# Ten weight blocks of a decoder trunk in products of seven, with the PSUM halves' role change moved

## The chip, the cores and the metric

The kernel runs on one core of a Trainium2 chip. The metric is the device time of one execution in microseconds, as the median of several runs. PE is TensorE (PEld its weight loads), DVE is VectorE, ACT is ScalarE, POOL is GpSimd, SP is SyncE, whose queue here issues the weight loads.

## The reference

One layer on 256 tokens of width 2048, all in float32. The input is normalised; one matrix `w_in` makes three branches' inputs and the gates; each branch's output of width 1024 goes through its own projection, is gated and summed; `w_out`, a scaled residual and a LayerNorm follow; then a SwiGLU feed-forward part (FFN) of width 5632 with its own residual and LayerNorm.

```python
x = layer_norm(x, ln_in_g, ln_in_b)
z = jnp.einsum('bsd,de->bse', x, w_in[l])
a_b, a_c, a_h, b_u, b_v, c_a, c_g, g = jnp.split(z, SPLITS, axis=-1)
gates = jax.nn.sigmoid(g + gate_bias[l]).reshape(bsz, s, N_BRANCH, D_MODEL)
y_a = short_gated_conv(a_b, a_c, a_h, conv_a_w[l])          # a_b * conv3(a_c * a_h)
y_b = chunked_spatial_gating(b_u, b_v, ...)                  # b_u * (W_group @ layer_norm(b_v) + b)
y_c = conformer_conv(c_a, c_g, ...)                          # silu(layer_norm(conv31(c_a * sigmoid(c_g))))
proj = jnp.einsum('bsnc,ncd->bsnd', ys, w_branch[l])
merged = jnp.sum(gates * proj, axis=2)
x = layer_norm(DEEPNORM_ALPHA * x + einsum(merged, w_out[l]), ln_mix_g[l], ln_mix_b[l])
h_gate, h_up = split(einsum(x, w_ffn_in[l]))
x = layer_norm(DEEPNORM_ALPHA * x + einsum(silu(h_gate) * h_up, w_ffn_out[l]), ...)
```

## The kernel before

**Products.** Activations stand transposed, so that 128 rows of the contraction (a k tile) lie on the partitions. The 256 tokens are two halves of 128 (`t`). Every float32 operand is split into a high and a low part (`whi`, `wlo` for weights, `th`, `tl` or `yh`, `yl` for activations): ACT casts the high part (L126), DVE subtracts it (L128). One product of a 128 x 128 activation block and a 128 x 512 weight block is three matmuls, high by high, high by low and low by high (L203 to L205, L247 to L249).

**Chunks and blocks.** The weights come in raw tiles of 512 KB, loaded on SP's queue in the order of a plan (L86 to L118). A chunk is 512 columns: a raw tile holds two k tiles, and a step of `gemm` (L220) uses one raw tile with both token halves, 12 matmuls. A block is 1024 columns as two halves `n`: a raw tile holds one k tile, and a plain step of `gemm_block` (L251) makes four products, again 12 matmuls. A block may have pairs: two raw tiles, that is a 2 x 2 of weight blocks, for which `split_pair` (L131) forms sums on DVE and splits seven weight operands, and PE makes seven products of them with sums of activations that `token_sums` (L780) has made before. Four of a pair's products go to four further PSUM banks, `shared`; after the last pair DVE forms from these what is added to each output (L291 to L296), and `total` (L805) adds it when the output is read. Pairs come after at most six plain steps (`LEAD`). Before the change only FFN blocks have pairs: three in those of `w_ffn_in`, two in those of `w_ffn_out` (called fo below).

**Loading ahead.** `pump` (L190) runs at each step: it loads up to five raw tiles ahead, splits three ahead, and takes up to two items from `background`, a list with the 31 taps of the long convolution on DVE (L536). There are four raw buffers and seven buffers for split weights.

**PSUM.** Eight banks form two halves of four. `acc_bank` takes from the first, `tp_bank` (transposes, L301) from the second, and `halves.reverse()` at the end of a chunk or block exchanges their roles. Transposes are mostly deferred by some steps with `defer` (L210), and `run_deferred` runs them when due.

**Skew.** Some chunks run the second token half a few steps behind the first (`SKEW` is 5): w_out's last chunk, and the first chunk of the FFN. When w_out's last chunk ends for a token half, `evac_o` (L760) adds the residual into `R`, takes statistics, normalises (L429), transposes (L305) and splits the result into `x2T`.

**Order of the stages.** cg, ca (twice), bv, bu, then for branch B four gate chunks and four projection chunks, then ac, ah, ab (twice), branch A and branch C in the same way, four w_out chunks, then the FFN in three parts. In branch C, `finish_c` (L558) normalises the convolution's output after the second gate chunk. `residual` (L749) loads a quarter of x again and normalises it into temporary tiles, one w_out chunk ahead of its use.

**Order of the instructions.** The code is written for a framework that orders each engine's instructions when the program is built, by priority of the code's order and by estimated times: an instruction whose operands are estimated late is passed by a later one. So taps or residual pieces can stand ahead of where the code has them. It also allocates the buffers and sets the waits.

Of the kernel before, what the change touches and what calls it, by code (L numbers as in the profile page):

```python
# [14 lines left out]
P = 128  # L15
D = 2048
# [24 lines left out]
H_PAIRS = 2  # L41
LEAD = 6
# [9 lines left out]
def trunk_kernel(ctx: ExitStack, tc: tile.TileContext, x, ln_in_g, ln_in_b, w_in, gate_bias,  # L52
# [78 lines left out]
    def split_pair(t0, t1):  # L131
# [3 lines left out]
        ts = ffp.tile([P, 3, NW], F32, name="tsum", bufs=1)  # L135
# [74 lines left out]
    def defer(fn, after=DEFER):  # L210

        deferred.append((clock[0] + after, fn))
# [38 lines left out]
    def gemm_block(key, xs, evac, combos=None):  # L251
# [7 lines left out]
        adds, shared = {}, None  # L259
# [7 lines left out]
        for s_, (kind, q, tile_) in enumerate(steps):  # L267
# [9 lines left out]
            else:  # L277
# [11 lines left out]
                if sp:  # L289
# [59 lines left out]
    for j in range(2):  # L349
        for nm, off in (("ac", OFF_AC), ("ah", OFF_AH), ("ab", OFF_AB)):  # L350
            plan_in(nm, off, j)
    plan_branch(BR_A)
    plan_branch(BR_C)
    for j in range(4):
# [25 lines left out]
    wT = cwp.tile([P, 8, P], F32, name="wT")  # L380
# [63 lines left out]

    xT = new_xt(act)
    def x_stats(t):
# [5 lines left out]
    def x_norm(t, q):  # L452
        mu, rs = x_ms[t]
        norm_transposed(xT, q, t, xt[t][:, cols(q)], mu, rs, PR_ING, PR_INB, new_tmp(), act=ACT_BLOCKS[t])
# [21 lines left out]
    b_ln = []  # L476

    def more_params():
# [12 lines left out]
        for b0 in range(0, 8, 4):  # L491
            tp = transpose4(sgw[:, b0:b0 + 4, :])
            nc.scalar.copy(out=wT[:, b0:b0 + 4, :], in_=tp)
        xin.close()
        brp = br.enter_context(tc.tile_pool(name="brp", bufs=1))
        for src in (sg_ln_g, sg_ln_b):
# [4 lines left out]
    defer(more_params)  # L501
# [81 lines left out]
    vt = {(t, j): brp.tile([P, NW], F32, name="gate", bufs=8) for t in range(NT) for j in range(2)}  # L583
# [18 lines left out]
    for j in range(2):  # L602
        def evac_bu(t, ps, j=j):
# [3 lines left out]
            def later():  # L607
                mx = tp_bank()
                for b in range(4):
                    nc.tensor.matmul(mx[:, b, :], lhsT=wT[:, 4 * j + b, :], rhs=vt[t, j][:, cols(b, P)],  # L610
# [13 lines left out]
    def branch(n, y, first, prepare=None, mT=None):  # L624
        gates = {}
        for j in range(4):
            gb = brp.tile([P, NW], F32, name="gb", bufs=2)
            o = n * D + j * NW
            nc.scalar.dma_start(out=gb, in_=gate_bias[0:1, o:o + NW].broadcast_to([P, NW]))

            def evac_g(t, ps, j=j, gb=gb):
                g = brp.tile([P, NW], F32, name="gate", bufs=8)
                nc.vector.tensor_tensor(out=g, in0=ps, in1=gb, op=ALU.add)
                nc.scalar.activation(out=g, in_=g, func=AF.Sigmoid)
                gates[j, t] = g

            gemm(("g", n, j), xT, evac_g)
            if j == 1 and prepare is not None:
                defer(prepare)
        if mT is not None:  # L640
            mT.extend(new_xt(act))
        for j in range(4):
            def evac_p(t, ps, j=j):
                m = merged[t][:, cols(j)]
                if first:
                    nc.vector.tensor_tensor(out=m, in0=ps, in1=gates[j, t], op=ALU.mult)
                else:
                    z = gates[j, t]
                    nc.vector.tensor_tensor(out=z, in0=ps, in1=z, op=ALU.mult)
                    nc.vector.tensor_tensor(out=m, in0=m, in1=z, op=ALU.add)  # L650
                if mT is not None:
                    defer(lambda: split_to(mT, 4 * j, t, transpose4(blocks(m))), 2)

            gemm(("p", n, j), y, evac_p)

    branch(BR_B, yb, True)


    ya = new_y()

    def branch_a_chunk(j):
        ac, st = {}, {}

        def evac_ac(t, ps):
            ac[t] = new_tmp()
            nc.scalar.copy(out=ac[t], in_=ps)

        gemm(("ac", j), xT, evac_ac)

        def evac_ah(t, ps):  # L670
            u = ac[t]
            nc.vector.tensor_tensor(out=u, in0=ps, in1=u, op=ALU.mult)

            def later():
                if t == 0:
                    st["pad"] = brp.tile([P, 4, KC - 1 + S], F32, name="pad", bufs=2)
                    nc.vector.memset(st["pad"][:, :, 0:KA - 1], 0.0)
                tp = transpose4(blocks(u))
                pad = st["pad"]
                nc.scalar.copy(out=pad[:, :, KA - 1 + t * P:KA - 1 + (t + 1) * P], in_=tp)  # L680
                if t < NT - 1:
                    return
                cv = st["cv"] = brp.tile([P, 4, S], F32, name="cv", bufs=2)
                for q in range(KA):
                    for b in range(4):
                        w_ = cw[:, 4 * j + b, KC + q:KC + q + 1]
                        if q == 0:
                            nc.vector.tensor_scalar(out=cv[:, b, :], in0=pad[:, b, 0:S], scalar1=w_,
                                                    scalar2=None, op0=ALU.mult)
                        else:  # L690
                            nc.vector.scalar_tensor_tensor(out=cv[:, b, :], in0=pad[:, b, q:q + S], scalar=w_,
                                                           in1=cv[:, b, :], op0=ALU.mult, op1=ALU.add)
            defer(later)

        gemm(("ah", j), xT, evac_ah)

        def evac_ab(t, ps):
# [3 lines left out]
            def later():  # L701
                tp = transpose4(blocks(a))
                z = blocks(a)
                nc.vector.tensor_tensor(out=z, in0=tp, in1=st["cv"][:, :, cols(t, P)], op=ALU.mult)
                split_to(ya, 4 * j, t, z)
            defer(later)

        gemm(("ab", j), xT, evac_ab)

    for j in range(2):  # L710
        branch_a_chunk(j)
    branch(BR_A, ya, False)
# [8 lines left out]
    branch(BR_C, yc, False, prepare_c, mT)  # L721
# [3 lines left out]
    R, x2T, xS, hS, kept = [], [], [], [], {}  # L725

    def open_ffn():
# [7 lines left out]
        hS.extend(ffp.tile([P, 4, H_PAIRS, P], F32R, name=f"hS{i}") for i in range(2))  # L735

    defer(open_ffn)
# [7 lines left out]
    lg2, lb2 = (a.rearrange("(o d) -> o d", o=1) for a in (ln_in_g, ln_in_b))  # L745
    for j in range(4):
        res = {}

        def residual(j=j, res=res):  # L749
            gj, bj = bcast(lg2, j), bcast(lb2, j)  # L750
            for t in range(NT):
                xr = new_tmp()
                nc.sync.dma_start(out=xr, in_=x2d[cols(t, P), cols(j)])
                nc.vector.scalar_tensor_tensor(out=xr, in0=xr, scalar=mv_in[t][:, 0:1], in1=gj,
                                               op0=ALU.subtract, op1=ALU.mult)
                nc.vector.scalar_tensor_tensor(out=xr, in0=xr, scalar=rs_in[t], in1=bj,
                                               op0=ALU.mult, op1=ALU.add)
                res[t] = xr

        def evac_o(t, ps, j=j, res=res):  # L760
            dst = R[t][:, cols(j)]
            nc.vector.scalar_tensor_tensor(out=dst, in0=res[t], scalar=ALPHA, in1=ps,
                                           op0=ALU.mult, op1=ALU.add)
            nc.vector.bn_stats(out=stm[t][:, j, :], in_=dst)
            if j == 3:
                mu, rs = mean_rstd(stm[t])
                for q in range(4):
                    r_ = R[t][:, cols(q)]
                    y = None
                    if 2 * q < S_PAIRS:  # L770
                        y = kept[t, q] = blocks(ffp.tile([P, NW], F32, name="a", bufs=4))
                    norm_transposed(x2T, q, t, r_, mu, rs, PR_MG, PR_MB, r_, y=y)
                if t == NT - 1:
                    for q in range((S_PAIRS + 1) // 2):
# [148 lines left out]
```

## Time and profile before

| | |
|---|---|
| median of 3 runs | 1572.71 us (1572.08 to 1574.39) |
| the profiled execution | 1571.79 us |
| its span | 1570.1 us |
| PE, PEld busy | 1535.4, 1260.3 us |
| DVE, ACT busy | 1211.1, 738.6 us |
| HBM over the span | 195 GB/s |

Busy times are shares of the span in which an engine had at least one instruction running. An instruction's duration reaches past the start of the next on the same engine, so what one costs in a full queue is the distance of starts, not the duration. A row like `x3` with one duration is several instructions on end.

### The profile page before, as it was taken

To read this page: it belongs to the slowest core of one execution; us is meant where nothing else is said; L and a number is where in the kernel's file an instruction comes from. 1 tells how busy PE (TensorE), PEld (TensorE's weight loads), DVE (VectorE), ACT (ScalarE), POOL (GpSimd) and SP (SyncE) were. 2 spreads that over 40 slices of the span, in tenths; PEclk is the share of its full clock that TensorE was granted. 3 is DMA by queue.
4 is the path that set the end of the run, shared out by engine and by line. 5 is a ranking of instruction groups with operands and counts; after the bars stand their busy time and mean duration, and the time that the engine had idled before them with its cause. 6 is when DMAs were issued, how large, how long until landed. Compare 5 with 4: busy or idle time off the path is not lost. (4 is left out here: it accounts for less than half of the span.)

```text
span 1570.1 us, 18638 instructions
## 1 busy us (share of the span) xinstructions
PE 1535.4 (98%) x6859; PEld 1260.3 (80%) x6859; DVE 1211.1 (77%) x1580; ACT 738.6 (47%) x837; POOL 16.7 (1%) x28
## 2 busy tenths in 40 slices
PE   7999999999999999999997999999999999999997
PEld 4888888888888888888886888788888878888885
DVE  7699999555565555677558689988999988889677
ACT  5444444434444444544335455554555554455441
POOL 1000000000000000000000000000000000000000
PEclk9999999999999999999998999999999999999998
DMA  6866666666666666685654666666665666666654
GB/s 196 291 189 187 187 182 195 207 193 188 188 187 195 204 199 194 194 281 184 207 163 137 200 188 200 202 205 202 198 190 185 200 191 201 204 191 205 214 175 147
DMA packets 131985, 308.12 MB, mean 196 GB/s; under 512 B 9908, under 2 KB 11028, under 8 KB 131894
## 3 DMA queue, kind: packets, MB, share of 16 engines
q1 hardware_dynamic: 125782, 295.38, 61.1%
q10 hardware_dynamic: 6112, 11.55, 2.5%
q8 instruction: 53, 0.87, 0.2%
q14 instruction: 38, 0.31, 0.1%
HBM read 304.80 MB, written 2.10 MB: 195 GB/s over the span
## 5 line engine op out<-in xcount | busy, mean ns | idle before, releaser
L128 DVE TENSOR_TENSOR wlo<-wraw,whi 128x1024 fp32r<-128x1024 f32 x551 | 669.3, 1220 | 297.4 <-ACT whi L126 294.8
L126 ACT CAST whi<-wraw 128x1024 fp32r<-128x1024 f32 x551 | 577.9, 1052 | 651.0 <-PE acc L205 429.6
L203 PE MATMUL acc<-whi,th 128*128 128x512 f32 x1136 | 445.5, 392 | 0.0
L204 PE MATMUL acc<-wlo,th 128*128 128x512 f32 x1136 | 443.2, 390 | 0.5 <-DVE wlo L128 0.5
L205 PE MATMUL acc<-whi,tl 128*128 128x512 f32 x1136 | 443.3, 390 | 0.0
L247 PE MATMUL acc<-whi,th 128*128 128x512 f32 x695 | 273.6, 394 | 1.2 <-ACT th L311 1.0
L248 PE MATMUL acc<-wlo,th 128*128 128x512 f32 x695 | 271.4, 391 | 0.0
L249 PE MATMUL acc<-whi,tl 128*128 128x512 f32 x695 | 271.0, 391 | 0.0
L205 PEld LDWEIGHTS acc<-whi,tl 128*128 128x128 f32 x1136 | 213.6, 188 | 45.2 <-DVE tl L312 0.6
L204 PEld LDWEIGHTS acc<-wlo,th 128*128 128x128 f32 x1136 | 213.8, 188 | 44.9 <-DVE wlo L128 0.9
L203 PEld LDWEIGHTS acc<-whi,th 128*128 128x128 f32 x1136 | 213.8, 188 | 43.6 <-ACT th L311 0.2
L247 PEld LDWEIGHTS acc<-whi,th 128*128 128x128 f32 x695 | 130.5, 188 | 30.1 <-ACT th L311 1.6
L249 PEld LDWEIGHTS acc<-whi,tl 128*128 128x128 f32 x695 | 130.4, 188 | 29.0 <-DVE tl L312 0.3
L248 PEld LDWEIGHTS acc<-wlo,th 128*128 128x128 f32 x695 | 130.6, 188 | 27.0
L126 ACT CAST whi<-tsum 128x1024 fp32r<-128x1024 f32 x74 | 61.7, 833 | 96.1 <-DVE tsum L138 79.0
L536 DVE SCALAR_TENSOR_TENSOR cv<-pad,cw,cv 128x256 f32<-128x256 f32 x240 | 100.2, 475 | 0.0
L128 DVE TENSOR_TENSOR wlo<-tsum,whi 128x1024 fp32r<-128x1024 f32 x74 | 70.5, 952 | 11.8 <-ACT whi L126 11.8
L203 PE MATMUL acc<-whi,yh 128*128 128x512 f32 x192 | 75.5, 393 | 0.0
L204 PE MATMUL acc<-wlo,yh 128*128 128x512 f32 x192 | 75.5, 393 | 0.0
L205 PE MATMUL acc<-whi,yl 128*128 128x512 f32 x192 | 74.7, 389 | 0.0
L138 DVE TENSOR_TENSOR tsum<-tsum,wraw 128x512 f32<-128x512 f32 x74 | 50.7, 686 | 0.6
L248 PE MATMUL acc<-wlo,xS 128*128 128x512 f32 x108 | 42.5, 394 | 1.1 <-DVE wlo L128 1.1
(147 smaller groups left out, 940.2 us busy)
## 6 DMA issues: line engine op xcount, KB each, us to landing
wraw<-in_w_in_dram SPq DMA_DIRECT2D x208, 512.0 KB, 4.3
wraw<-in_w_ffn_in_dram SPq DMA_DIRECT2D x176, 512.0 KB, 4.4
wraw<-in_w_ffn_out_dram SPq DMA_DIRECT2D x88, 512.0 KB, 4.5
wraw<-in_w_branch_dram SPq DMA_DIRECT2D x48, 512.0 KB, 4.5
wraw<-in_w_out_dram SPq DMA_DIRECT2D x32, 512.0 KB, 3.9
gb<-in_gate_bias_dram ACTq DMA_DIRECT2D x12, 256.0 KB, 4.2
tmp<-in_x_dram SPq DMA_DIRECT2D x8, 256.0 KB, 8.1
x<-in_x_dram SPq DMA_DIRECT2D x2, 512.0 KB
```

Of the source, the lines that this page charges most:

```text
L126: nc.scalar.copy(out=hi, in_=t)
L128: nc.vector.tensor_tensor(out=lo, in0=t, in1=hi.bitcast(F32), op=ALU.subtract)
L138: nc.vector.tensor_tensor(out=out, in0=a, in1=b, op=ALU.add)
L203: nc.tensor.matmul(ps, lhsT=xh[:, k, ts], rhs=hi[:, kk, :], start=first, stop=False)
L204: nc.tensor.matmul(ps, lhsT=xh[:, k, ts], rhs=lo[:, kk, :], start=False, stop=False)
L205: nc.tensor.matmul(ps, lhsT=xl[:, k, ts], rhs=hi[:, kk, :], start=False, stop=last)
L247: nc.tensor.matmul(ps, lhsT=ah, rhs=bh, start=first, stop=False)
L248: nc.tensor.matmul(ps, lhsT=ah, rhs=bl, start=False, stop=False)
L249: nc.tensor.matmul(ps, lhsT=al, rhs=bh, start=False, stop=last)
L536: nc.vector.scalar_tensor_tensor(out=cv[:, b, :], in0=pad[:, b, q:q + S], scalar=w_, in1=cv[:, b, :], op0=ALU.mult, op1=ALU.add)
```

## The change

`gemm` exchanges the roles of the PSUM halves before it evacuates the second token half, no longer after the last deferred work. The gates, ac, ah, ab and the first two chunks of w_out become blocks of 1024 columns with two pairs each; the projections become blocks without pairs. Gates and projections alternate by half (gates 0, projections 0, gates 1, projections 1). Token sums are made of the input (`xTS`) early in the first chunk and of merged (`mTS`) late in branch C; the parameters' transposes come four steps later. Deferred work that needs PSUM banks is held while a block's `shared` banks are in use. `finish_c` runs in the first gate block of branch C. The residual's x is loaded straight into `R`, whose memory follows that of the branches, in four pieces 7, 9, 11 and 13 steps after branch C's end. The buffers for gates are four instead of eight.

```diff
+SUMS_AT = 5
+X_PAIRS = 2
...
-    def run_deferred():
-        due = [f for at, f in deferred if at <= clock[0]]
-        deferred[:] = [d for d in deferred if d[0] > clock[0]]
-        for f in due:
-            f()
+    def run_deferred(held=False):
+        due = [d for d in deferred if d[0] <= clock[0] and not (held and d[2])]
+        deferred[:] = [d for d in deferred if d not in due]
+        for d in due:
+            d[1]()
...
                 if ii == n - 1:
+                    if t == NT - 1:
+                        halves.reverse()
                     evac(t, ps[t])
             clock[0] += 1
             run_deferred()
         for i in range(n):
             split_t.pop(first_tile + i)
-        halves.reverse()
...
                     adds = {(0, 1): c1, (1, 1): v, (0, 0): r, (1, 0): w}
+                    free_at = s_ + 3
             clock[0] += 1 if kind == "one" else 2
-            run_deferred()
+            run_deferred(shared is not None and not 0 < free_at <= s_ and not last)
...
-        for j in range(4):
-            add_chunk(("g", n, j), wi, OFF_G + n * D + j * NW, 0, 16)
-        for j in range(4):
-            add_chunk(("p", n, j), w_branch[0, n], j * NW, 0, 8)
+        for b in range(2):
+            add_block(("g", n, b), wi, OFF_G + n * D + 2 * b * NW, 0, 16, X_PAIRS)
+            add_block(("p", n, b), w_branch[0, n], 2 * b * NW, 0, 8)
...
+    for nm, off in (("ac", OFF_AC), ("ah", OFF_AH), ("ab", OFF_AB)):
+        add_block(nm, wi, off, 0, 16, X_PAIRS)
...
+    add_block(("o", 0), w_out[0], 0, 0, 16, X_PAIRS)
+    for j in (2, 3):
         add_chunk(("o", j), w_out[0], j * NW, 0, 16)
...
-    defer(more_params)
+    defer(lambda: token_sums(xTS, 0, x_kept[0], x_kept[1], X_PAIRS), SUMS_AT, False)
+    defer(more_params, SUMS_AT + 1)
...
+    def branch(n, y, first, mT=None):
+        for b in range(2):
+            gates = {}
+            gb = [brp.tile([P, NW], F32, name="gb", bufs=2) for _ in range(2)]
+            for i in range(2):
+                o = n * D + (2 * b + i) * NW
+                nc.scalar.dma_start(out=gb[i], in_=gate_bias[0:1, o:o + NW].broadcast_to([P, NW]))
+
+            def evac_g(i, t, h, ps, add):
+                g = gates[t, h] = brp.tile([P, NW], F32, name="gate", bufs=4)
+                nc.vector.tensor_tensor(out=g, in0=total(ps, add), in1=gb[h], op=ALU.add)
                 nc.scalar.activation(out=g, in_=g, func=AF.Sigmoid)
+
+            gemm_block(("g", n, b), xT, evac_g, xTS)
...
+            gemm_block(("p", n, b), y(), evac_p)
...
+    defer(prepare_c, 3)
+    branch(BR_C, lambda: yc, False, mT)
...
+    def residual(j):
+        gj, bj = bcast(lg2, j), bcast(lb2, j)
+        for t in range(NT):
+            xr = res[t, j] = R[t][:, cols(j)]
+            nc.sync.dma_start(out=xr, in_=x2d[cols(t, P), cols(j)])
+            nc.vector.scalar_tensor_tensor(out=xr, in0=xr, scalar=mv_in[t][:, 0:1], in1=gj,
+                                           op0=ALU.subtract, op1=ALU.mult)
+            nc.vector.scalar_tensor_tensor(out=xr, in0=xr, scalar=rs_in[t], in1=bj,
+                                           op0=ALU.mult, op1=ALU.add)
...
     for j in range(4):
+        defer(lambda j=j: residual(j), 7 + 2 * j, False)
+    gemm_block(("o", 0), mT, lambda i, t, h, ps, add: evac_o(t, h, ps, add), mTS)
+    for j in (2, 3):
+        gemm(("o", j), mT, lambda t, ps, j=j: evac_o(t, j, ps), skew=SKEW if j == 3 else 0)
```

## Rows read from the trace of the kernel before

**Rows 1.** The page: span, busy times (part 1), granted clock by slice (part 2).

```profile
span 1570.1 us, 18638 instructions
...
PE 1535.4 (98%) x6859; PEld 1260.3 (80%) x6859; DVE 1211.1 (77%) x1580; ACT 738.6 (47%) x837; POOL 16.7 (1%) x28
...
PEclk9999999999999999999998999999999999999998
```

**Rows 2.** Windows: length; busy us (count) of PE, PEld, DVE, ACT, POOL; PEclk, DMA share, GB/s.

```profile
495.79:561.07 65.28, 65.28 (x290) 54.05 (x289) 33.04 (x31) 28.43 (x30) 0.00 (x0) 1.00 0.67 203
...
740.46:784.89 44.43, 44.43 (x202) 36.87 (x200) 27.84 (x31) 17.84 (x18) 0.00 (x0) 1.00 0.63 198
```

**Rows 3.** Waits of PE: who waited for whom, us in total, times, longest.

```profile
PE acc L305 <- DVE R L429: 9.9, 2, 9.1
PE acc L305 <- DVE tmp L429: 8.7, 6, 3.3
PE acc L420 <- DVE zero L417: 1.3, 1, 1.3
```

**Rows 4.** PE's timeline around w_out's end: start us, us, instruction, idle before it.

```profile
831.02 0.40 PE L205 MATMUL acc<-whi,tl 128*128 128x512 f32 x1
840.55 3.65 PE L305 MATMUL acc<-ident,R 128*128 128x128 f32 x16 [9.13 <-DVE R L429]
843.85 0.78 PE L203 MATMUL acc<-whi,th 128*128 128x512 f32 x1
```

**Rows 5.** Windows, the same columns, of the stretch with the lower clock.

```profile
834.50:844.70 10.20, 4.15 (x18) 4.08 (x19) 8.57 (x16) 2.98 (x8) 1.63 (x2) 0.50 0.50 154
```

**Rows 6.** Windows: the FFN gate block with three pairs, fo's second block.

```profile
1104.47:1146.36 41.89, 41.89 (x185) 34.37 (x183) 38.55 (x48) 21.90 (x24) 0.00 (x0) 1.00 0.67 208
...
1321.30:1363.51 42.21, 42.21 (x187) 34.91 (x186) 35.19 (x42) 20.37 (x21) 0.00 (x0) 1.00 0.63 199
```

**Rows 7.** DVE's timeline: four taps, three adds, three differences, each on end.

```profile
142.11 1.66 DVE L536 SCALAR_TENSOR_TENSOR cv<-pad,cw,cv 128x256 f32<-128x256 f32 x4
...
973.75 1.88 DVE L810 TENSOR_TENSOR tmp<-acc,tmp 128x512 f32<-128x512 f32 x3
...
1036.64 3.49 DVE L128 TENSOR_TENSOR wlo<-wraw,whi 128x1024 fp32r<-128x1024 f32 x3
```

**Rows 8.** Windows: from branch B to the FFN's first chunk.

```profile
204.00:860.00 656.00, 646.09 (x2912) 535.22 (x2911) 423.64 (x538) 285.70 (x320) 5.26 (x8) 0.99 0.65 195
```

**Rows 9.** Windows: branch B's gates up to the last tap.

```profile
204.34:268.80 64.46, 64.46 (x302) 53.74 (x301) 64.27 (x121) 28.73 (x32) 0.00 (x0) 1.00 0.64 190
```

**Rows 10.** The taps' line from 204.34 us on: count, duration ns, first and last start.

```profile
L536 DVE SCALAR_TENSOR_TENSOR cv<-pad,cw,cv x81: 461/474/482, 204.4 to 268.3; 128x256 f32<-128x256 f32 x81
```

**Rows 11.** Groups by line: the residual's first instruction and its wait.

```profile
L754 DVE SCALAR_TENSOR_TENSOR tmp<-tmp,mvin 128x512 f32<-128x512 f32 x8 | 5.9, 749 | 8.4 <-DMA tmp<-in_x_dram 8.4
```

**Rows 12.** Windows: FFN up block with mix residuals, fo's first blocks of two parts.

```profile
973.90:1017.75 43.85, 42.70 (x185) 34.21 (x183) 41.31 (x52) 20.81 (x25) 0.00 (x0) 1.00 0.62 194
1017.75:1062.26 44.51, 44.45 (x203) 36.29 (x202) 38.41 (x46) 24.73 (x29) 0.00 (x0) 1.00 0.65 213
...
1273.87:1321.30 47.43, 45.40 (x204) 36.09 (x202) 41.60 (x51) 23.61 (x27) 0.00 (x0) 1.00 0.64 201
```

**Rows 13.** DVE's timeline at w_out's end.

```profile
829.63 0.68 DVE L312 TENSOR_TENSOR tl<-a,th 128x512 fp32r<-128x512 f32 x1
...
833.10 1.29 DVE L312 TENSOR_TENSOR tl<-tmp,th 128x512 fp32r<-128x512 f32 x2
...
834.90 1.22 DVE L128 TENSOR_TENSOR wlo<-wraw,whi 128x1024 fp32r<-128x1024 f32 x1
...
837.94 1.16 DVE L128 TENSOR_TENSOR wlo<-wraw,whi 128x1024 fp32r<-128x1024 f32 x1
```

**Rows 14.** Waits of ACT in 1255 to 1294 us.

```profile
ACT whi L126 <- DMA wraw<-in_w_ffn_out_dram: 8.2, 4, 3.1
```

**Rows 15.** Windows: the stretch with the most DMA traffic.

```profile
40.00:80.00 40.00, 40.00 (x182) 33.21 (x181) 25.76 (x32) 19.65 (x21) 0.00 (x0) 1.00 0.86 282
```

More of the change, by code (lines that the diff above doesn't have):

```diff
@@ L580, in new_y @@
         return (brp.tile([P, 8, S], F32R, name="yh"), brp.tile([P, 8, S], F32R, name="yl"))
-    vt = {(t, j): brp.tile([P, NW], F32, name="gate", bufs=8) for t in range(NT) for j in range(2)}
+    vt = {(t, j): brp.tile([P, NW], F32, name="gate", bufs=4) for t in range(NT) for j in range(2)}
     bst = stats_tile("bst", 2)
@@ L622, in trunk_kernel, with total @@
     merged = [brp.tile([P, D], F32, name=f"merged{t}") for t in range(NT)]
[L624 to L633, printed above, removed]
-                nc.scalar.activation(out=g, in_=g, func=AF.Sigmoid)
[L635 to L643, printed above, removed]
+    def total(ps, add):
+        if add is None:
+            return ps
+        c = new_tmp()
+        nc.vector.tensor_tensor(out=c, in0=ps, in1=add, op=ALU.add)
+        return c
@@ new lines, in to_left, with go, evac_p @@
+    def to_left(dst, sums, k, t, a, after):
+        def go():
+            tp = transpose4(blocks(a))
+            if k > 0:
+                split_to(dst, 4 * k, t, tp)
+                return
+            y = kept[t] = blocks(new_tmp())
+            nc.scalar.copy(out=y, in_=tp)
+            split_to(dst, 0, t, y)
+            if t == NT - 1:
+                defer(lambda: token_sums(sums, 0, kept[0], kept[1], H_PAIRS), 1, False)
+        defer(go, after)
+    kept = {}
+    def branch(n, y, first, mT=None):
[8 more added lines that the diff above has]
+                nc.vector.tensor_tensor(out=g, in0=total(ps, add), in1=gb[h], op=ALU.add)
+                nc.scalar.activation(out=g, in_=g, func=AF.Sigmoid)
+            gemm_block(("g", n, b), xT, evac_g, xTS)
+            if b == 1 and mT is not None:
+                mT.extend(new_xt(act))
+                mTS.extend(new_sums())
+                later = late[:]
+                late.clear()
+                for i, f in enumerate(later):
+                    f(DEFER + i)
+            def evac_p(i, t, h, ps, add):
+                j = 2 * b + h
@@ new lines, in move, with evac_ac @@
+                    def move(after):
+                        to_left(mT, mTS, j, t, m, after)
+                    if b == 0:
+                        late.append(move)
+                    else:
+                        move(DEFER + i)
+            gemm_block(("p", n, b), y(), evac_p)
+    late, mTS = [], []
+    branch(BR_B, lambda: yb, True)
+    ya = new_y()
+    ac, pads, cvs = {}, {}, {}
+    def evac_ac(i, t, h, ps, add):
+        a = ac[t, h] = brp.tile([P, NW], F32, name="gate", bufs=4)
+        if add is None:
+            nc.scalar.copy(out=a, in_=ps)
+        else:
+            nc.vector.tensor_tensor(out=a, in0=ps, in1=add, op=ALU.add)
@@ new lines, in trunk_kernel, with evac_ah, later @@
+    gemm_block("ac", xT, evac_ac, xTS)
+    def evac_ah(i, t, h, ps, add):
+        u = ac[t, h]
+        nc.vector.tensor_tensor(out=u, in0=total(ps, add), in1=u, op=ALU.mult)
+        def later():
+            if h not in pads:
+                pads[h] = brp.tile([P, 4, KC - 1 + S], F32, name="pad", bufs=2)
+                nc.vector.memset(pads[h][:, :, 0:KA - 1], 0.0)
+            pad = pads[h]
+            tp = transpose4(blocks(u))
+            nc.scalar.copy(out=pad[:, :, KA - 1 + t * P:KA - 1 + (t + 1) * P], in_=tp)
+            if t < NT - 1:
+                return
+            cv = cvs[h] = brp.tile([P, 4, S], F32, name="cv", bufs=2)
+            for q in range(KA):
+                for b in range(4):
+                    w_ = cw[:, 4 * h + b, KC + q:KC + q + 1]
+                    if q == 0:
+                        nc.vector.tensor_scalar(out=cv[:, b, :], in0=pad[:, b, 0:S], scalar1=w_,
+                                                scalar2=None, op0=ALU.mult)
+                    else:
+                        nc.vector.scalar_tensor_tensor(out=cv[:, b, :], in0=pad[:, b, q:q + S], scalar=w_,
+                                                       in1=cv[:, b, :], op0=ALU.mult, op1=ALU.add)
+        defer(later, DEFER + i)
@@ L698, in evac_ab @@
+    gemm_block("ah", xT, evac_ah, xTS)
+    def evac_ab(i, t, h, ps, add):
+        a = total(ps, add)
+        if add is None:
             a = new_tmp()
             nc.scalar.copy(out=a, in_=ps)
[L701 to L708, printed above, removed]
@@ L710, in trunk_kernel, with later @@
-    for j in range(2):
-        branch_a_chunk(j)
-    branch(BR_A, ya, False)
+        def later():
+            tp = transpose4(blocks(a))
+            z = blocks(a)
+            nc.vector.tensor_tensor(out=z, in0=tp, in1=cvs[h][:, :, cols(t, P)], op=ALU.mult)
+            split_to(ya, 4 * h, t, z)
+        defer(later, DEFER + i)
+    gemm_block("ab", xT, evac_ab, xTS)
+    branch(BR_A, lambda: ya, False)
     while background:
@@ L745, in trunk_kernel @@
     lg2, lb2 = (a.rearrange("(o d) -> o d", o=1) for a in (ln_in_g, ln_in_b))
-    for j in range(4):
[L747 to L774, printed above, removed]
-                        defer(lambda q=q: token_sums(xS, 2 * q, kept[0, q], kept[1, q], min(2, S_PAIRS - 2 * q)), 6 + q)
-        defer(residual)
-        gemm(("o", j), mT, evac_o, skew=SKEW if j == 3 else 0)
@@ L780, in token_sums @@
[L780 to L792 removed]
+    res = {}
@@ new lines, in evac_o @@
+    def evac_o(t, j, ps, add=None):
+        dst = R[t][:, cols(j)]
+        nc.vector.scalar_tensor_tensor(out=dst, in0=dst, scalar=ALPHA, in1=total(ps, add),
+                                       op0=ALU.mult, op1=ALU.add)
+        nc.vector.bn_stats(out=stm[t][:, j, :], in_=dst)
+        if j < 3:
+            return
+        mu, rs = mean_rstd(stm[t])
+        for q in range(4):
+            r_ = R[t][:, cols(q)]
+            y = None
+            if 2 * q < S_PAIRS:
+                y = kept[t, q] = blocks(ffp.tile([P, NW], F32, name="a", bufs=4))
+            norm_transposed(x2T, q, t, r_, mu, rs, PR_MG, PR_MB, r_, y=y)
+        if t == NT - 1:
+            for q in range((S_PAIRS + 1) // 2):
+                defer(lambda q=q: token_sums(xS, 2 * q, kept[0, q], kept[1, q], min(2, S_PAIRS - 2 * q)), 6 + q, False)
```

123 lines of the change are left out of this document (35 added, 88 removed).

## The prediction

> **What bounds the kernel now.** I began with the page's busy times and slices: PE is busy for 1535.4 of 1570.1 us, DVE for 77%, and PE's granted clock falls only in the 22nd slice and the last [rows 1]. So TensorE sets the time wherever it does not wait, and the question is what its work costs and where it waits. For the cost I took a stretch in which nothing else happens, the last three gate chunks of branch A: 3 x 96 = 288 matmuls in 65.28 us, 226.7 ns each (the 290 in the row counts neighbours at the edges). Two chunks of w_out with eight transposes take 44.43 us; less 192 x 0.2267 = 43.52 that leaves 0.11 us for a transpose [rows 2]. The reader is to see there that PE is busy to the last hundredth while DVE is busy half the time.
>
> For the waits I asked who holds PE up: 9.9 us for the residual R in two waits, 8.7 us for the first normalisation, and no other group of waits over 1.3 us [rows 3]. The 9.1 us wait has its own rows: the last matmul of w_out's fourth chunk starts at 831.02, then nothing until the transposes of R at 840.55, and the first FFN matmul at 843.85 [rows 4]. [...]
>
> **What goes.** A pair of k tiles over two token halves and two column halves takes seven products in place of eight; a product is three matmuls. A block of 16 k tiles and 1024 columns thus has 12 x 12 + 2 x 21 = 186 matmuls instead of 192. Ten blocks get two pairs: six of gates, ac, ah, ab, and the first half of w_out. That is 60 matmuls x 0.2267 = **13.6 us** off the engine that sets the end. The projections only become wider blocks without pairs, with the same matmuls. Weight bytes are the same.
>
> The same shape runs already: the second fo block of the second FFN part has 16 k tiles, two pairs and an added total at the end. It takes 42.21 us with 186 matmuls, 42.16 by the rate above, so PE does not wait although DVE is busy for 35.19 us [rows 6]. That is my row for a new block.
>
> **What DVE gets.** By issue spacing (three adds in 1.88 us, three 1024-wide differences in 3.49, four taps in 1.66) an add holds DVE for 0.60 us, a difference 1.14, a tap 0.395 [rows 7]. A pair costs four adds, three wide differences and a narrow one, 6.4 us, where two plain tiles cost 2.3: 8.3 us more per block. The seven-product sums cost 4 x 0.60, the totals 4 x 0.60. Each block gets 13.1 us more, the ten 131 us. From 204 to 860 us DVE is now busy for 424 of 656 us [rows 8], so on average it fits; what matters is the places:
> - Branch B: from 204.34 to 268.80 DVE is busy for 64.27 of 64.46 us, and PE loses nothing there [rows 9]. What fills it are 81 convolution taps, 81 x 0.395 = 32 us [rows 10], which the planner has moved into gaps: the code emits two per step, the trace shows four. A gate block without taps asks for 31 us plus 3 to 5 for what the previous stage left, of 42; a projection block for 12 of 22. The four blocks leave about 10 us each, so the taps end with the branch. Cost 0 to 3 us, taken 1.
> - First gate block of branch C: finishing the conformer convolution moves from the third gate chunk to the third step of this block. It needs about 10 us of DVE (eight scalings, eight differences and products, two normalisations), queued ahead of the first pair's split; before the pair lie 16.3 us of plain steps plus 1.8 of transposes, and DVE must do 4.8 (last evacuation), 3.4 (splits), 10 and 6.4 = 24.6 us by then, of which the pair's last 4 may come while its products run. Cost 24.6 - 18.1 - 4.1 = 2.4; the range is 0 to 4; taken 2.
> - First half of w_out: all four residual pieces now fall into this block, and since they land in R, whose memory is free only when the branches are done, they can't be taken ahead as now. Sixteen DVE instructions at some 0.67 are 10.7 us, with 2.4 for splitting merged; the block asks for 31 + 10.7 + 2.4 + 2.4 (statistics) = 47 us of 43. The plain chunk behind it has slack and three tiles are split ahead (8 us), so 0 to 5, taken 2. DVE already waits 8.4 us on the x loads in eight instructions; queued behind such a wait would be splits [rows 11].
> - The other seven blocks: between the fo block above, 0.05 us over, and the first fo block of the same part, 47.43 us less 42.16 and 16 transposes (1.8), which is 3.5 over [rows 6, 12]; its twin in part one is 0.6 over. I take 0.15 each, 1 us together, as most FFN blocks lie at that end.
>
> Sum of new stalls: 1 + 2 + 2 + 1 = **6 us** (range 1 to 15). The token sums at the start put about 2.5 us on a DVE that feeds PE's first steps, while the parameter transposes move later: 0.5 (0 to 2).
>
> [...]
>
> **What the moved role change does.** In a chunk, the PSUM halves now change roles before the evacuation of the second token half. Before, the transposes of R's second half took the banks of the half that the next chunk accumulates in; with both needing the same four banks, the first FFN chunk could not begin until those transposes had been read. Now they take the half of the chunk just ended, and the FFN chunk's banks held only the first token half's transposes. With a skew of five steps, 30 matmuls of the first token half need nothing of the second; with seven split buffers up to 42 can go: 6.8 to 9.5 us. Their data are there: the first half's low parts end between 830.3 and 834.4, and weight splits follow at 834.9 to 837.9 [rows 13]. So most of the 9.1 us fills: I take 7. [...] Together **8.5 us**. Bounds: 0 if the planner keeps the order, 11 if all fills. What is late next is the second half's chain on DVE and ACT, behind which the next chunk's splits stand.
>
> Elsewhere the moved role change costs nothing: no other evacuation transposes at once, and deferred ones fall into the first steps, where banks are free. Keeping the gates in four buffers instead of eight is free too, as a block of projections (22 us) lies between two blocks of gates.
>
> **Sum.** -13.6 - 8.5 + 6 + 0.5 = -15.6. The profiled execution took 1571.79 us (span 1570.1 and 1.7 around it), so 1556.2; it lies 0.9 below the median of the runs shown, so I predict **1557**. By its own bounds the likeliest case reaches from 1550 (fill 10.5, stalls 2) to 1562.
>
> **Rivals.**
> 1. *The wait for R stays.* The planner places the transposes ahead of the FFN matmuls, so PE's queue waits as before. For it: the other wait for R, 0.8 us [rows 3], fell among matmuls of the same chunk that stood behind it. Against: those matmuls show that it does put one token half's products into the other's gaps. Gain lost 8.5: 1565.5.
> 2. *DVE's bursts cost more than I take.* Branch C's block 4, w_out's 5 plus 2 in the next chunk, branch B 3: 14 in place of 6: 1565. For it: the gate-up block at 974 us, where eight mix-residual instructions came on top, took 43.85 for 41.48 us of matmuls [rows 12]. Against: most FFN blocks.
> 3. *Slower: weights late at every pair.* Pairs take two raw tiles at once and hold them through the adds, with four raw buffers. In the first fo block of part two ACT stood 8.2 us for w_ffn_out in four waits [rows 14], and PE lost 3.5. If the new blocks meet that and lose 3.5 each, 35 us come in place of 6: 1586. It decides from 2.8 us a block (13.6 + 8.5 + 6, over ten) on. For it: bursts of x and broadcasts in w_out's block add 4 MB to 8.4 MB in 43 us, 290 GB/s, where the highest stretch had 282 [rows 15]. Against: 208 GB/s with no loss in the three-pair gate block [rows 6].
> 4. *The removed products do not show.* DVE is full in branch B, and PE paces to it: the taps' 32 us and the ten blocks' 131 cost what the matmuls save, with the R wait left: about 1572.
>
> [...]
>
> **How the numbers follow.** Likeliest 0.53, rival 1 0.20, rival 2 0.12, rival 3 0.09, rival 4 0.06. The range 1550 to 1570 holds the first three, 0.85, less their tails. Within 0.2% (3.1 us, what a measurement of this kernel can tell from no change) is 0.06, nearly all of it rival 4. Slower is rival 3 and a little of 4: 0.11. Faster is the rest, 0.83.
>
> **What would show it.** 6453 matmuls of weights instead of 6513; new blocks of 42.2 us in place of pairs of chunks of 43.5; FFN matmuls between w_out's last and the transposes of R, and no half clock near 830; DVE busy above 80% in the branches with PE at its pace. Wrong would be: waits of PE on weight differences inside the new blocks of more than 1 us each, above all in branch C's first and in w_out's; or an idle PE of 9 us ahead of R's transposes still.

## The result and the profile after

The changed kernel takes **1556.8 us** (1555.20 to 1557.72, four runs); the kernel before, run beside it, 1572.87. The ratio is 0.9896, 95% interval 0.9878 to 0.9913: 16 us faster. 1557 was predicted. The profiled execution took 1555.20 us, 16.59 less than the one of before.

The page of the changed kernel (span, busy times, granted clock by slice; it answers [rows 1], as the views below answer the rows that they name):

```profile
span 1553.5 us, 18790 instructions
...
PE 1522.1 (98%) x6799; PEld 1247.2 (80%) x6799; DVE 1340.1 (86%) x1792; ACT 771.1 (50%) x885; POOL 16.4 (1%) x28
...
PEclk9999999999999999999999999999999999999999
```

60 PE instructions fewer, 13.3 us less PE time, and 129 us more DVE time. In line numbers of the changed kernel the low parts are L130 (before L128), a pair's adds L140, chunk matmuls L205 to L207, block matmuls L251 to L253, transposes L310 (L305), added totals L656, the normalisation L432 (L429), the residual's two steps L816 and L818 (L754 and its neighbour), its evacuation L823 and L825.

Windows of the changed kernel (columns as in [rows 2]): the first gate block of branch B, the second gate block of branch A, the first of branch C, w_out's block, w_out's third and fourth chunk, the FFN's first chunk, and all from branch B to there:

```profile
203.86:249.86 46.00, 45.23 (x211) 37.40 (x210) 44.53 (x75) 21.92 (x24) 0.00 (x0) 1.00 0.55 174
...
533.11:575.27 42.16, 42.16 (x188) 34.91 (x187) 32.28 (x37) 20.23 (x21) 0.00 (x0) 1.00 0.61 194
...
597.24:641.19 43.95, 43.95 (x203) 36.61 (x202) 41.31 (x55) 24.51 (x29) 0.00 (x0) 1.00 0.58 181
729.13:773.33 44.20, 44.20 (x204) 36.35 (x202) 40.66 (x53) 20.20 (x23) 0.00 (x0) 1.00 0.71 230
773.33:800.47 27.14, 23.70 (x98) 19.08 (x96) 19.88 (x25) 9.03 (x9) 0.00 (x0) 0.94 0.52 166
800.47:825.08 24.61, 23.84 (x114) 19.43 (x113) 17.96 (x27) 12.56 (x19) 1.66 (x2) 1.00 0.66 207
825.08:850.19 25.11, 24.60 (x114) 19.36 (x113) 23.46 (x46) 16.36 (x28) 1.63 (x2) 1.00 0.45 138
204.00:850.00 646.00, 640.04 (x2877) 526.79 (x2876) 548.43 (x741) 320.92 (x369) 4.72 (x8) 1.00 0.62 197
```

A gate block with nothing beside it takes 42.16 us: 186 matmuls at 0.2267, no loss. DVE is busy for 548 of 646 us, where it was 424 of 656 [rows 8]. One window stands out: the third chunk of w_out is a plain chunk of 96 matmuls (21.76 us) and takes 27.14, at a mean clock of 0.94. I call what a stage takes beyond its matmuls (0.2267 us) and transposes (0.111) its stall.

PE's waits, in the changed kernel (answers [rows 3]):

```profile
PE acc L310 <- DVE tmp L432: 9.3, 6, 3.4
PE acc L206 <- DVE wlo L130: 3.4, 1, 3.4
...
PE acc L252 <- DVE wlo L130: 1.2, 2, 0.8
PE acc L310 <- DVE R L432: 1.1, 2, 0.8
```

PE's timeline of the changed kernel in 784 to 842 us (answers [rows 4]):

```profile
784.21 0.39 PE L205 MATMUL acc<-whi,th 128*128 128x512 f32 x1
788.04 0.50 PE L206 MATMUL acc<-wlo,th 128*128 128x512 f32 x1 [3.44 <-DVE wlo L130]
...
789.32 0.58 PE L205 MATMUL acc<-whi,th 128*128 128x512 f32 x1
789.71 0.63 PE L206 MATMUL acc<-wlo,th 128*128 128x512 f32 x1
...
792.69 0.43 PE L207 MATMUL acc<-whi,tl 128*128 128x512 f32 x1
...
833.55 0.40 PE L206 MATMUL acc<-wlo,th 128*128 128x512 f32 x1
834.29 2.02 PE L310 MATMUL acc<-ident,R 128*128 128x128 f32 x16 [0.34 <-DVE R L432]
```

Two things are to be seen. The transposes of R at 834.29 wait 0.34 us instead of 9.13 and take 2.02 instead of 3.65: 38 FFN matmuls, from 825.08 to 833.55, now stand ahead of them. And PE waits 3.44 us for a low part in w_out's third chunk; shortly after, its matmuls lie 0.43 us apart, not 0.23, until 792.7, and the granted clock in 789.4 to 792.6 was 0.50.

What held that low part is in DVE's timeline of the changed kernel, same place:

```profile
776.59 1.42 DVE L816 SCALAR_TENSOR_TENSOR R<-R,mvin,tmp 128x512 f32<-128x512 f32 x2 [1.80 <-DMA tmp<-in_ln_in_g_dram]
779.46 1.41 DVE L818 SCALAR_TENSOR_TENSOR R<-R,rsin,tmp 128x512 f32<-128x512 f32 x2 [1.46 <-DMA tmp<-in_ln_in_b_dram]
780.79 0.69 DVE L823 SCALAR_TENSOR_TENSOR R<-R,tmp 128x512 f32<-128x512 f32 x1
...
786.18 0.67 DVE L823 SCALAR_TENSOR_TENSOR R<-R,tmp 128x512 f32<-128x512 f32 x1
786.77 1.22 DVE L130 TENSOR_TENSOR wlo<-wraw,whi 128x1024 fp32r<-128x1024 f32 x1
```

The residual's fourth piece waits for its two broadcasts (scale, then shift). Behind it stand the evacuations of w_out's block, which fill 780.8 to 786.8, and only then comes the split that PE needs.

**Where 16.6 us went, by stages.** Matmuls -13.6; w_out's fourth chunk and the FFN's first two 71.69 for 81.66, -9.97; w_out's third chunk +5.38; the gates of branch B +1.08, of branch A +1.01; w_out's block +0.23; ab +0.1; the FFN behind these with its tail -0.4; the start -0.4. Sum -16.6.

### The profile page after: what moved, and what is told of

It reads as the page before. It is cut to its first block, busy times and chain, and to the rows that moved or that the text cites. A ratio compares the mean times of both kernels' runs of the same rounds, so it can differ in the third digit from the quotient of the medians.

```text
span 1553.5 us, 18790 instructions
## 1 busy us (share of the span) xinstructions
PE 1522.1 (98%) x6799; PEld 1247.2 (80%) x6799; DVE 1340.1 (86%) x1792; ACT 771.1 (50%) x885; POOL 16.4 (1%) x28
## 5 line engine op out<-in xcount | busy, mean ns | idle before, releaser
L128 ACT CAST whi<-wraw 128x1024 fp32r<-128x1024 f32 x551 | 577.2, 1051 | 539.3 <-PE acc L253 152.3
L130 DVE TENSOR_TENSOR wlo<-wraw,whi 128x1024 fp32r<-128x1024 f32 x551 | 666.4, 1220 | 127.7 <-ACT whi L128 124.1
L251 PE MATMUL acc<-whi,th 128*128 128x512 f32 x1235 | 485.7, 393 | 2.1 <-ACT th L316 1.0
L252 PE MATMUL acc<-wlo,th 128*128 128x512 f32 x1235 | 481.6, 390 | 0.0
L253 PE MATMUL acc<-whi,tl 128*128 128x512 f32 x1235 | 481.1, 390 | 0.0
L251 PEld LDWEIGHTS acc<-whi,th 128*128 128x128 f32 x1235 | 231.9, 188 | 52.0 <-ACT th L316 1.8
L253 PEld LDWEIGHTS acc<-whi,tl 128*128 128x128 f32 x1235 | 231.7, 188 | 50.3 <-DVE tl L317 0.3
L252 PEld LDWEIGHTS acc<-wlo,th 128*128 128x128 f32 x1235 | 232.0, 188 | 47.5
L206 PE MATMUL acc<-wlo,th 128*128 128x512 f32 x496 | 194.6, 393 | 3.4 <-DVE wlo L130 3.4
L205 PE MATMUL acc<-whi,th 128*128 128x512 f32 x496 | 195.7, 395 | 0.2 <-ACT th L316 0.2
L207 PE MATMUL acc<-whi,tl 128*128 128x512 f32 x496 | 194.4, 393 | 0.0
L128 ACT CAST whi<-tsum 128x1024 fp32r<-128x1024 f32 x114 | 95.3, 836 | 145.6 <-DVE tsum L140 122.6
L130 DVE TENSOR_TENSOR wlo<-tsum,whi 128x1024 fp32r<-128x1024 f32 x114 | 108.5, 952 | 12.5 <-ACT whi L128 12.5
L206 PEld LDWEIGHTS acc<-wlo,th 128*128 128x128 f32 x496 | 93.8, 189 | 23.5 <-DVE wlo L130 4.1
L207 PEld LDWEIGHTS acc<-whi,tl 128*128 128x128 f32 x496 | 93.8, 189 | 20.2 <-DVE tl L317 0.4
L205 PEld LDWEIGHTS acc<-whi,th 128*128 128x128 f32 x496 | 93.7, 189 | 20.1 <-ACT th L316 0.8
L140 DVE TENSOR_TENSOR tsum<-tsum,wraw 128x512 f32<-128x512 f32 x114 | 78.1, 685 | 0.6
L251 PE MATMUL acc<-whi,yh 128*128 128x512 f32 x192 | 75.7, 394 | 0.0
L253 PE MATMUL acc<-whi,yl 128*128 128x512 f32 x192 | 74.7, 389 | 0.0
L140 DVE TENSOR_TENSOR tsum<-wraw 128x512 f32<-128x512 f32 x57 | 39.2, 688 | 29.9 <-DMA wraw<-in_w_in_dram 21.1
```

The costliest lines, as they stand in the source:

```text
L128: nc.scalar.copy(out=hi, in_=t)
L130: nc.vector.tensor_tensor(out=lo, in0=t, in1=hi.bitcast(F32), op=ALU.subtract)
L140: nc.vector.tensor_tensor(out=out, in0=a, in1=b, op=ALU.add)
L205: nc.tensor.matmul(ps, lhsT=xh[:, k, ts], rhs=hi[:, kk, :], start=first, stop=False)
L206: nc.tensor.matmul(ps, lhsT=xh[:, k, ts], rhs=lo[:, kk, :], start=False, stop=False)
L207: nc.tensor.matmul(ps, lhsT=xl[:, k, ts], rhs=hi[:, kk, :], start=False, stop=last)
```

## The experiments

Each edit is against the changed kernel unless it says otherwise. Ratios are to the kernel before, run on the same chip (1572.3 to 1573.4 us).

**The role change undone** (e1).

```diff
-                    if t == NT - 1:
-                        halves.reverse()
                     evac(t, ps[t])
...
+        halves.reverse()
```

> The changed kernel with the role change back at the end of a chunk. Theory (the moved role change lets first-half FFN matmuls run during the wait for R): the 9 us wait and the half clock return, the three stages w_out's last chunk to FFN's second lengthen by 10.0 us, the time goes from 1556.8 to 1566-1568. Rival (the new block order or the residual loaded into R freed the FFN's start): stays at 1557 within 2 us.

1569.08 us, ratio 0.9976 (0.9968 to 0.9985). PE's waits in this kernel:

```profile
PE acc L309 <- DVE R L431: 9.9, 2, 9.1
...
PE acc L206 <- DVE wlo L130: 5.4, 3, 4.9
```

The wait for R is back to the tenth [rows 3]. w_out's fourth chunk takes 36.96 us for 24.61, the FFN's first gives 3.0 back (22.08 for 25.11): 9.3 us. Another 2.55 come from w_out's third chunk, where PE waits 4.9 us here; the medians differ by 12.3.

**The role change alone** (e2: the kernel before, with the same two lines moved).

> The kernel before with only the role change moved. Theory: the wait for R fills, 10 us less, 1562 to 1564, no wait of PE on R over 1.5 us. Rival (it needs the other edits, for instance R written in place or the earlier memory change): 1572 to 1573.

1562.82, ratio 0.9941 (0.9929 to 0.9952): 9.5 us by the medians. The same three stages take 71.69 us, to the hundredth as in the changed kernel, and the wait for R is the same:

```profile
PE acc L306 <- DVE R L430: 1.1, 2, 0.8
```

So this part is worth 9.97 us, and it needs nothing of the rest.

**No pairs** (e3: the ten blocks stay blocks, all tiles plain).

```diff
-            add_block(("g", n, b), wi, OFF_G + n * D + 2 * b * NW, 0, 16, X_PAIRS)
+            add_block(("g", n, b), wi, OFF_G + n * D + 2 * b * NW, 0, 16)
```

and so for ac, ah, ab and w_out's first half.

> The changed kernel with no pairs in the ten new blocks (the blocks, their order and the token sums stay): 60 matmuls more, 13.6 us, less what pairs cost in stalls. Theory (pairs bring 2 us of stalls in branches B and A, and w_out's 5 us stall comes of pair sums holding the temporary buffers that the last residual piece needs): 1556.8 + 13.6 - 7 = 1562 to 1565. If w_out's stall is not tied to the pairs: 1567 to 1570. Rival 4 (the removed products do not show): 1557.

1563.49, ratio 0.9944 (0.9932 to 0.9956). The first gate block of branch B and w_out's third chunk in this kernel:

```profile
203.78:250.06 46.28, 46.28 (x217) 38.61 (x216) 46.15 (x90) 19.16 (x21) 0.00 (x0) 1.00 0.59 180
...
784.76:806.52 21.76, 21.76 (x97) 18.02 (x96) 15.34 (x18) 8.65 (x9) 0.00 (x0) 1.00 0.69 219
```

w_out's third chunk takes 21.76 us, no loss; the first gate blocks of branches B and A lose 0.10 and 0.11 for 1.17 and 1.01. So these stalls come with the pairs, and the 13.6 us that the pairs take off PE show as 6.7 in the medians.

**Neither** (e6: both edits above).

> The changed kernel with neither pairs in the ten blocks nor the moved role change; block form, order, token sums and residual pieces stay. If the two parts add up: 1563.5 + 10 = 1572 to 1575, level with the kernel before. If undoing the role change costs what it cost beside the pairs, 12: 1575 to 1577.

1572.02, ratio 0.9985 (0.9976 to 0.9994). What is left of the change (blocks, the new order of gates and projections, four buffers for gates, x straight into R) is worth 1 to 4 us and costs nothing.

**The fourth residual piece later** (e4). Theory: the wait of 3.44 us comes from the fourth piece's broadcasts, which get their buffers only as the block's temporaries come free; five steps later DVE does the evacuations first.

```diff
-        defer(lambda j=j: residual(j), 7 + 2 * j, False)
+        defer(lambda j=j: residual(j), (7, 9, 11, 18)[j], False)
```

> The changed kernel with the fourth residual piece asked for at 18 instead of 13 steps, inside w_out's third chunk. Theory (DVE stands 3.3 us for that piece's broadcasts, which came late for want of temporary buffers, with the splits queued behind; PE then waits 3.4 us and loses clock): the chunk falls from 27.1 to 22-22.5 us and the time to 1551-1553. Rival (w_out's raw tiles come late because x and the broadcasts share the DMA engines): within 1.5 us of 1556.8.

1548.54, ratio 0.9848 (0.9835 to 0.9861): the fastest, ahead of both kernels, and by more than I expected. Its window of w_out's third chunk, and two lines of DVE there:

```profile
771.49:793.47 21.98, 21.98 (x98) 17.95 (x96) 17.95 (x23) 7.26 (x8) 0.00 (x0) 1.00 0.65 204
```

```profile
780.35 1.21 DVE L130 TENSOR_TENSOR wlo<-wraw,whi 128x1024 fp32r<-128x1024 f32 x1
781.48 1.41 DVE L816 SCALAR_TENSOR_TENSOR R<-R,mvin,tmp 128x512 f32<-128x512 f32 x2
```

The split comes ahead of the piece, the piece waits for nothing, and the mean clock is 1.00 where it was 0.94. The stage gives 5.2 us back, the medians differ by 8.3. Between the two profiled executions, 7.9 us apart, the rest lies elsewhere: 1.8 us up to the end of the first chunk, which the edit does not touch, and 0.9 in the FFN.

**Both again, on one chip** (e10: the changed kernel; e11: the fourth piece later).

> The changed kernel as it is, beside the next one on the same chip. If the wait of 3.4 us in w_out's third chunk comes in every run, 1555 to 1558 and the chunk at 26 to 28 us; if it hangs on when the broadcasts land, another length of the chunk, between 21.8 and 27 us, and the time with it.

> The kernel with the residual's fourth piece at 18 steps again, on the same chip as the changed kernel. If the late piece is worth what its chunk shows, it is 5.2 us below the changed kernel; what was measured in another call was 8.2 below. Expected 1549 to 1551.

1559.38 (0.9906, 0.9889 to 0.9923) and 1549.45 (0.9842, 0.9825 to 0.9859). The changed kernel again, PE and then DVE:

```profile
790.96 0.80 PE L206 MATMUL acc<-wlo,th 128*128 128x512 f32 x1 [6.44 <-DVE wlo L130]
```

```profile
781.05 1.42 DVE L816 SCALAR_TENSOR_TENSOR R<-R,mvin,tmp 128x512 f32<-128x512 f32 x2 [4.35 <-DMA tmp<-in_ln_in_g_dram]
```

The broadcast was issued at 773.9 us where it was at 772.0 before, and took 7.1 us to land where it took 4.5; the chunk took 30.19 us where it took 27.14, and the stall is 8.4. So the loss hangs on when a DMA lands, between 5.4 and 8.4 us in the two profiles, and the late piece takes all of it away. In this pair the medians differ by 9.9 us and the profiled executions by 9.7, of which 8.4 lie in the chunk.

**Buffers of its own for the broadcasts** (e5): the scale and shift of the residual go to the FFN's "a" tiles, idle here, instead of the shared temporaries; the pieces stay where they are.

> The changed kernel with the residual's broadcasts in four idle FFN buffers instead of the temporary ones; the pieces are asked for at 7, 9, 11 and 13 steps as in the change. Theory (the fourth piece's broadcasts were issued late because pair sums and totals held the eight temporary buffers): w_out's third chunk falls from 27.1 to 22-23 us as with the late piece, 1548 to 1551. Rival (the piece simply asks too much of DVE and DMA at that place, whatever the buffers): 1555 to 1558.

A miss: 1558.3, ratio 0.9908 (0.9894 to 0.9923), no faster than the changed kernel. Windows of w_out's block and its third chunk, then PE's wait and what stood ahead of it on DVE and ACT:

```profile
727.76:779.63 51.87, 46.34 (x203) 37.63 (x202) 44.06 (x58) 19.45 (x23) 0.00 (x0) 0.93 0.64 202
779.63:801.43 21.80, 21.80 (x97) 18.02 (x96) 17.30 (x21) 10.20 (x10) 0.00 (x0) 1.00 0.67 225
```

```profile
PE acc L252 <- DVE wlo L130: 6.3, 3, 5.5
```

```profile
747.46 0.75 DVE L816 SCALAR_TENSOR_TENSOR R<-R,mvin,a 128x512 f32<-128x512 f32 x1 [3.29 <-DMA a<-in_ln_in_g_dram]
...
770.14 0.69 DVE L296 TENSOR_TENSOR tmp<-acc,tmp 128x512 f32<-128x512 f32 x1 [2.44 <-ACT tmp L295]
```

```profile
768.58 1.05 ACT L128 CAST whi<-wraw 128x1024 fp32r<-128x1024 f32 x1 [3.70 <-DMA wraw<-in_w_out_dram]
```

The third chunk loses nothing, and the fourth piece's broadcasts are issued at 760.2 and 761.5 us, not at 772.0 and 772.4: so the temporaries did hold the late broadcasts. But all four pieces now fall into the block, which loses 7.9: DVE has 44.06 us of work there, and PE 43.9. The time came out as the rival had it, that the block has no room for four pieces; the trace shows more of the cause. DVE's wait of 3.3 us at 747 holds up no matmul. PE's one wait in the block, 5.5 us up to 775.1, is for a split that DVE makes at 773.86 although ACT had cast its tile by 763.6. Ahead of it on DVE stand the fourth piece and the pair's totals (L296), these wait 2.44 us for a copy on ACT (L295), and ACT had stood 3.70 us for a weight tile. So it is again what waits at the head of a queue; why that tile came late is not shown.

**Extra DVE work in the FFN** (e7, on e4): one more 512-wide add, into a tile that nobody reads, in each of the FFN's 37 pairs. By spacing 0.60 us each, by duration 0.69.

> The late-piece kernel (1548.5) with one more add of 512 columns on DVE in each of the 37 FFN pairs, overwritten at once. If DVE pays the issue spacing of 0.60: a gate or up block has 3.5 us free and takes 1.8, so 0 to 3 us in all, 1548 to 1552. If it pays the duration of 0.69 with nothing overlapped: such a block would need 41.7 + 2.1 of 41.9, 1.9 us over in each of nine, 1564 to 1568.

1555.21, ratio 0.9882 (0.9868 to 0.9895), 5 to 7 us above e4; by its total between the two theories. But from the FFN's first up block to the first fo block of its last part, where the adds are, the profiled execution takes 640.2 us for 636.6 in e4 (636.7 in e11): 3.6 us, close to the 0 to 3 by spacing and far from the 15 to 20 by durations. The rest lies where no add runs, such as 1.5 us in branch A's first gate block. The up block with the mix residual and a plain gate block, of e4 and then of e7:

```profile
950.77:995.14 44.37, 42.76 (x184) 34.19 (x183) 41.94 (x53) 21.19 (x25) 0.00 (x0) 1.00 0.64 196
...
1081.47:1123.36 41.89, 41.89 (x185) 34.37 (x183) 37.89 (x47) 22.34 (x24) 0.00 (x0) 1.00 0.66 204
```

```profile
953.86:999.06 45.20, 43.42 (x184) 33.82 (x183) 44.15 (x57) 21.27 (x25) 0.00 (x0) 1.00 0.62 191
1085.99:1127.88 41.89, 41.89 (x185) 34.37 (x184) 40.03 (x50) 21.07 (x23) 0.00 (x0) 1.00 0.63 198
```

Where DVE had room, three adds more cost nothing (41.89 both). Where it was full, they cost 0.8 us. The 41.7 us of the expectation are durations added up, 10 x 1.22 + 3 x 7.1 + 12 x 0.68 [rows 13], 7.1 being a pair's five at 0.68 and three at 1.22, for a block in which DVE was busy for 38.55 us [rows 6]. By durations the plain block would have gone over as well (those of its 49 instructions add up to 43.3 us, in 41.89); it did not. In e7 a 512-wide add takes 0.69 us and the next instruction starts 0.60 after its start (1067.14 and 1067.74 us), so that a part of its duration overlaps with the next. That durations add up is not what the runs show.

**The mix residual's last two pieces later** (e8, on e4): 32 steps later, out of the FFN's second up block.

> The late-piece kernel with the mix residual's last two pieces moved from the FFN up block at 958 us, which asks for more than it has (2.9 us of waits), to the second fo block of the part. Theory (same mechanism: DVE over its block's length): 2 to 2.5 us less, 1545.5 to 1547. Rival (that block's wait comes of its raw tiles): 1548 to 1549.

1551.6, ratio 0.9862 (0.9849 to 0.9876), no gain. The up block and the first fo block of part one, in e8 (for the up block in e4 see above; the fo block took 44.17 there):

```profile
951.50:993.40 41.90, 41.90 (x185) 34.37 (x184) 36.21 (x43) 22.69 (x27) 0.00 (x0) 1.00 0.62 194
993.40:1040.93 47.53, 45.36 (x204) 36.09 (x202) 41.19 (x50) 23.80 (x27) 0.00 (x0) 1.00 0.62 198
```

The up block gains 2.5 us and the next block loses 3.4.

**Five buffers for split weights instead of seven** (e9, on e4). The step on branch C had foretold 2 us, and nothing came. Theory: the framework splits as far ahead as buffers allow, not three tiles, and so puts the pair ahead of `finish_c`. That is the order in the changed kernel, where the pair's last split comes when `finish_c` has made its first two scalings (L598):

```profile
607.14 0.99 DVE L598 TENSOR_SCALAR tmp<-acc,prm 128x256 f32<-128x256 f32 x2
608.04 0.68 DVE L130 TENSOR_TENSOR wlo<-tsum,whi 128x512 fp32r<-128x512 f32 x1
```

With five buffers it should turn round, and the block lose 2 to 4 us.

> The kernel with the residual's fourth piece at 18 steps, with five buffers for split weights instead of seven. Theory: branch C's first gate block lost nothing because the pair's sums and splits were made up to seven tiles ahead, before finish_c; with five buffers they come after it, and the block loses 2 to 4 us where it lost 0.02; the fill ahead of R's transposes shrinks from 38 matmuls to at most 30, 1 to 2 us; and the FFN's pairs, four split tiles each, lose 1 us or more a block. Together 10 us or more: 1560 to 1580. Rival: three tiles ahead, as the code asks, were enough and the order of the code is what runs; then branch C's block stays under 0.5 us and the whole within 2 us of 1548.5.

1557.62, ratio 0.9901 (0.9884 to 0.9917): 8 to 9 us slower than with seven, but not there. The first gate block of branch C, w_out's third chunk and the FFN's first, in this kernel:

```profile
593.54:637.47 43.93, 43.93 (x204) 36.63 (x203) 41.05 (x55) 24.95 (x29) 0.00 (x0) 1.00 0.57 180
770.10:793.23 23.13, 22.05 (x97) 17.94 (x96) 19.47 (x26) 8.42 (x8) 0.00 (x0) 1.00 0.70 230
819.05:846.51 27.46, 25.55 (x113) 19.26 (x114) 26.04 (x49) 17.74 (x32) 1.63 (x2) 1.00 0.45 131
```

Branch C's block loses nothing either, so the order is not what spared it. DVE's timeline in e9 shows why:

```profile
607.17 0.99 DVE L598 TENSOR_SCALAR tmp<-acc,prm 128x256 f32<-128x256 f32 x2
608.08 0.68 DVE L604 TENSOR_TENSOR yl<-tmp,yh 128x512 fp32r<-128x512 f32 x1
...
614.26 0.68 DVE L130 TENSOR_TENSOR wlo<-tsum,whi 128x512 fp32r<-128x512 f32 x1
```

`finish_c` is now interleaved with the pair's sums and splits, and takes 8.4 us (eight scalings at 0.455, eight more at 0.60), not 10. The pair's last operand is ready at 614.9; PE reaches that product at 615.7. Even with five buffers it just fits. What the two buffers are worth lies elsewhere: fewer FFN matmuls fit ahead of R's transposes (27 for 38), the stages from w_out's third chunk to the FFN's first lose 4.7 us more together than in e4, and the last two chunks of the FFN another 4 to 5; the FFN between them is 1 us shorter.

## Why the prediction was right

The total was right and each of its four terms came out within 2 us; the largest of the stalls lay in another place, by another mechanism.

- **Removed matmuls, -13.6: right.** 60 fewer, new blocks at 42.16 us, projections unchanged. DVE became busy for 129 us more, where I had added up 131.
- **The role change, -8.5: right mechanism, undersized.** It is 9.97. I let 7 of the 9.1 us fill; both waits for R together fell from 9.9 to 1.1, so 8.8 filled, 38 matmuls of the 30 to 42 that I had counted. The other 1.5 of the 8.5 were the 16 transposes: 3.3 us up to the next matmul before [rows 4], at a granted clock of 0.50 [rows 5], less 16 x 0.11. That came out: they take 1.8 us up to the next matmul (834.29 to 836.07) at a clock of 1.00. The chain named as late next shows in the FFN's first chunk, at 1.57 us of stall for 0.72.
- **New stalls, 6: 7.8 in the profiled execution, but not where I put them.** Branch B's 1 became 1.08. Branch C's 2 became 0: I had `finish_c` queued ahead of the pair's split, and most of it came behind it; and where the two interleave (e9), I had sized `finish_c` 1.6 us too long and put the evacuations behind the block's start, which began 1.9 ahead of it. The seven others, 1 together, cost 1.1, nearly all in branch A's first. w_out's block, 2 (0 to 5): the block itself lost 0.23, and the chunk behind it 5.4 to 8.4.
- **The step that failed** is its sentence "The plain chunk behind it has slack and three tiles are split ahead". The slack was there (DVE is busy for 17.95 of 21.98 us in e4), but in DVE's order the fourth piece's wait for two broadcasts (1.80 and 1.46 us, 4.35 in e10) stood ahead of the split, with 6 us of evacuations between them. I had named splits queued behind the wait for x; it was the broadcasts, whose buffers are the temporaries that the pairs and their totals hold (e3 and e5: without either, the chunk loses nothing). And I counted a wait at its length only: after PE had stood for 3.4 us its granted clock also fell to 0.50 for 3.4 us (789.3 to 792.7), which turned 3.4 into 5.4.
- **Token sums at the start, +0.5: about nothing.** The first chunk and what lies ahead of it are 0.4 us shorter, but 0.5 could not be told there: the first matmul of weights starts at 13.15 us in e4 and at 15.14 in e11, the same kernel.

**The rivals.** The wait for R did not stay (rival 1); e1 shows its price, 9.3 in its own stages. DVE's bursts (rival 2, 14 for 6) came in part, and mostly in one place, the chunk behind w_out's block: 7.8 in the first profile, 11.6 in e10, where the broadcast was late. Late weights at every pair (rival 3) did not come: no new block loses more than 1.7 us in either profile of the changed kernel. That the products do not show (rival 4) was half true with the role change undone: e6 to e1 gives 2.9 us of the 13.6 by the medians (6.6 between the profiled executions), and w_out's third chunk alone lost 7.9 there.

That 1557 came out is in part luck: a larger gain at R (1.5) was offset by larger stalls (1.8), above all at w_out's third chunk, and that stall varies: the same kernel took 1559.38 in e10.

## What to carry to other kernels

When an engine gets more work, ask not only whether it has room in a stage but what stands at the head of its queue when the next stage needs it: here one instruction that waited for a DMA (1.80 us, and 4.35 in e10) held up the splits queued behind it, and moving its piece five steps back was worth 8 to 10 us. Buffers that a new scheme holds longer can delay whatever shares their pool, as they did two broadcasts here (issued at 772.0 and 772.4 us, with buffers of their own at 760.2 and 761.5). And where two halves of PSUM exchange roles at the end of a stage, see which of the next stage's work needs the banks that the last evacuation takes: doing the exchange ahead of that evacuation, two lines, gave 10 us here.

## What the runs showed of the hardware

Behind waits of 3.4 us (changed kernel), 4.9 (e1) and 6.4 (e10) inside a dense stream, PE's matmuls lay some 0.43 us apart, not 0.23, for 3.4, 5.7 and 3.6 us. In the changed kernel the granted clock there was 0.50 (789.4 to 792.6 us), and its mean over the chunk 0.94; in e10 the mean over the chunk was 0.89. I had counted on a lower clock only around the 9.1 us wait of before (0.50 in 834.5 to 844.7 us [rows 5]). The landing time of one 256 KB broadcast was 4.5 us in one profile of the changed kernel and 7.1 in the next; with that and a later issue, the chunk behind it took 3 us more.
